# Decoder layer on one core: where four row sums and their split parts stand, and the residual rows' scaling, two blocks a step

## The chip, the cores and the metric

The kernel runs on one core of a Trainium2 chip. The metric is the device time of one execution in microseconds (us), the median of several runs. The engines are TensorE (PE, matrix products; PEld is its weight load), VectorE (DVE), ScalarE (ACT), GpSimd (POOL) and SyncE (SP, which issues most transfers).

## The reference

One layer of a decoder on 512 positions of 1024 channels, all in float32: layer norm of the input; one input projection that gives attention queries, a latent key/value, an index query, key and weights, three convolution inputs and two gates; attention over the 128 keys that the index scores choose; a gated short convolution; the two branches, gated and summed, through an output projection; layer norm; a gated feed-forward part with its own short convolution and a per-layer embedding; layer norm.

```python
h = layer_norm(x, ln_emb_g, ln_emb_b)
proj = h @ w_in
score = einsum(relu(einsum(q_idx, k_idx) * 1/8), w_idx * 8**-0.5)   # per query and key
sel = top_k(score, 128)                                             # causal keys only
...
merged = sigmoid(g_att + b0) * (att @ w_br_att) + sigmoid(g_conv + b1) * (conv_y @ w_br_conv)
h = layer_norm(2**0.25 * h + merged @ w_o, ln1_g, ln1_b)
...
```

## The kernel before

**Number format.** Every product is made as three products of a high and a low part. The high part is a rounding copy by ACT (`wh`, line 76, for weights), the low part a subtraction, raw minus high, by DVE or POOL (`wl`, line 143). A weight chunk (512 KB, 128x1024) is loaded by SP into one of four raw buffers, split three steps ahead of its use (`lead`), and used by 24 PE instructions.

**Order.** The whole order is written out by hand. `self.steps` is a list of functions; `run` goes through it. For step i it first calls `advance(i)` (loads and splits of the weight chunks that are due), then the functions in `self.preps[i]`, then the step itself; from step `side_from` on, it then gives DVE some rounds of top-k. Each engine does its instructions in the order in which they are issued here, so the list sets every engine's queue. The tiles of tag `k4` share 28 buffers of 4 KB a partition, those of tag `k2` eight of 2 KB, and PSUM has eight banks, taken in turn.

**Steps 0 to 19.** Steps 0 to 3 project the index queries (`qi`), a quarter each. Step 1 also turns the small keys (`ckT`, `kiT`, line 416) that `small_norm` in `start` makes (`kn` and `cn`, lines 400 to 406, on DVE, after a power on POOL, line 395). Steps 2 to 5 each make the index scores of two heads: PE `raw` (line 166), ACT `rl` (584), DVE `score` (586, one multiply-add for each head and block). Steps 4 and 5 also finish two chunks of the first convolution group, of which half was made in `start`; step 5 multiplies them (`cvu`, 764) and convolves (ACT taps 754, POOL sums 755, `cvt`). `at_first` is 6: step 6 is the group's third chunk (`cvy`, 771; its parts `cvT`, 773 and 774), steps 7 to 10 are the attention queries q0 to q3 (`qa`), steps 11 to 19 three more convolution groups of three chunks each. Steps 14 and 16 also make the latent keys and values, step 18 starts attention. From step 5 on DVE runs top-k (596 to 601) between the steps, four to two rounds a step.

**Steps 20 on.** Attention's eight parts, gates, and the branch products (`branch`, `br`) share these steps. From step 30 on the gates are made by a block product that needs sums and differences of quarter blocks of `h`: `hblock` holds the four blocks (rows half by channel half, 128x1024 each), `first_sum(n)` makes the four sums in place on POOL (line 795, tile `hx`), `first_parts(n)` their high part on ACT and low part on POOL (`fsh`, 801; `fsl`, through `low`, 143). The gate steps read these parts as `self.hsum`, first in step 31. POOL also issues transfers that add weights in DRAM (line 1329), from step 20 on, each behind a small token.

**The end of the attention part.** `at_slot` numbers the steps from 20 on, leaving out some of the gate steps. Its entries 18 to 23 are the branch products (2,1), (0,0), (1,0), (2,0), (3,1), (3,0): the pair is (channel group, branch). Each makes two PSUM banks of 12 matmuls; DVE multiplies each by its gate (902), and for branch 0 adds the other branch (904), after which ACT and POOL split the sum (`mT`, 906 and 907). The residual rows (`hr`, four blocks of 128 rows) are loaded at entry 17; `res_affine(b)` multiplies block b by `ge` and adds `be` (lines 1028 and 1029, two DVE passes over 128x1024). In the last branch step's preparation, `onto` copies the first half of each block into a PSUM bank by ACT (`wo`, 1047), and the output projection (`wo_half0`, 916 to 918) accumulates onto these banks, block by block.

Of the kernel before, what the change touches and what calls it, by code (L numbers as in the profile page):

```python
# [85 lines left out]
class Kern:  # L86
# [425 lines left out]
    def plan(self):  # L512
# [277 lines left out]
        def first_sum(n):  # L790

            b11, b12, b21, b22 = (self.hblock[g, h] for g in range(2) for h in range(2))
            to, x, y, op = ((b11, b11, b12, OP.subtract), (b12, b22, b12, OP.subtract),
                            (b22, b11, b22, OP.add), (b21, b22, b21, OP.subtract))[n]
            return lambda: nc.gpsimd.tensor_tensor(to, x, y, op=op)

        def first_parts(n):
            def f():
                b = self.hblock[((0, 0), (0, 1), (1, 1), (1, 0))[n]]
                hi, lo = (self.k4(f"fs{x}{n}", F32R, (P, 4, 256)) for x in "hl")  # L800
                nc.scalar.copy(hi, b)
                self.low("p", lo, b, hi)
                self.hsum[n] = [(hi[:, c], lo[:, c]) for c in range(4)]
            return f
# [157 lines left out]
        at_first = len(self.steps)  # L962
# [7 lines left out]
        at_slot, pairs = [], {}  # L970
        for i, o in enumerate(order):
# [24 lines left out]
            n = att_at.get(i)  # L996
# [1 line left out]
                fn = with_att(n, fn)  # L998
            step(fn, [w] if o[0] != "G" or k else pairs[j][:2])
        for n in range(4):  # L1000
            self.preps.setdefault((1, 1, 2, 3)[n], []).append(lambda n=n: first_sum(n)())
            self.preps.setdefault((3, 5, 7, 8)[n], []).append(first_parts(n))
        self.side_from = at_first - 1


# [20 lines left out]
        def res_affine(b):  # L1026
            t, (ge, be) = self.hr[b], self.res_affine
            nc.vector.tensor_tensor(t, t, ge, op=OP.mult)
            nc.vector.tensor_tensor(t, t, be, op=OP.add)
# [7 lines left out]
        self.preps.setdefault(at_slot[17], []).append(res_rows)  # L1037
        self.preps.setdefault(at_slot[19], []).append(res_scale)
        for b in range(NB):
            self.preps.setdefault(at_slot[(20, 21, 22, 22)[b]], []).append(lambda b=b: res_affine(b))  # L1040

        self.zps = {}

# [428 lines left out]
        n = len(those)  # L1472
# [323 lines left out]
```

## Time and profile before

| | |
|---|---|
| median of 3 runs | 749.81 us (749.81 to 750.61) |
| profiled execution, its own time | 750.77 us |
| its span | 748.8 us |
| mean granted TensorE clock | 0.993 |
| PE, DVE, ACT, POOL busy | 97%, 83%, 57%, 36% of the span |

The span runs from the first to the last instruction; the execution's own time has some 2 us around it. Timeline rows give the start in us from the span's start, the duration, engine, line, operation, written tile <- read tiles, shapes and count; in square brackets stands how long the engine was idle before and what ended that. An engine that waits inside an instruction shows a longer duration. A row of the windows gives a stretch, its length, then the busy time of each engine with its count of instructions, the granted clock of PE (1.00 is full speed), the DMA share and GB/s.

### The profile page before, as it was taken

To read this page: it belongs to the slowest core of one execution; us is meant where nothing else is said; L and a number is where in the kernel's file an instruction comes from. 1 tells how busy PE (TensorE), PEld (TensorE's weight loads), DVE (VectorE), ACT (ScalarE), POOL (GpSimd) and SP (SyncE) were. 2 spreads that over 40 slices of the span, in tenths; PEclk is the share of its full clock that TensorE was granted. 3 is DMA by queue.
4 is the path that set the end of the run, shared out by engine and by line. 5 is a ranking of instruction groups with operands and counts; after the bars stand their busy time and mean duration, and the time that the engine had idled before them with its cause. 6 is when DMAs were issued, how large, how long until landed. Compare 5 with 4: busy or idle time off the path is not lost. (4 is left out here: it accounts for less than half of the span.)

```text
span 748.8 us, 12201 instructions
## 1 busy us (share of the span) xinstructions
PE 726.5 (97%) x4399; PEld 640.0 (85%) x4399; DVE 621.7 (83%) x1045; ACT 426.3 (57%) x718; POOL 271.8 (36%) x332
## 2 busy tenths in 40 slices
PE   8989989999999999989999999999999999999995
PEld 5978868888888998768888999999999998888884
DVE  5879899985566665889998899999998899987787
ACT  5627274437766654333575666777777665665630
POOL 4345399526575841320101233433332212111002
PEclk9999999999999999999999999999999999999999
DMA  9362369869999999376998998889899869998761
GB/s 354 115 262 71 106 191 343 294 205 252 250 232 190 206 253 379 130 256 216 305 377 263 313 281 251 242 250 250 227 239 250 240 197 224 267 263 245 251 211 57
DMA packets 61867, 178.02 MB, mean 238 GB/s; under 512 B 7232, under 2 KB 7360, under 8 KB 61424
## 3 DMA queue, kind: packets, MB, share of 16 engines
q1 hardware_dynamic: 43968, 140.56, 53.6%
q0 software_dynamic: 16976, 35.27, 26.6%
q10 hardware_dynamic: 864, 1.43, 0.6%
q8 instruction: 34, 0.56, 0.3%
q14 instruction: 25, 0.20, 0.1%
HBM read 171.46 MB, written 70.78 MB: 324 GB/s over the span
## 5 line engine op out<-in xcount | busy, mean ns | idle before, releaser
L143 DVE TENSOR_TENSOR wl<-wr,wh 128x1024 fp32r<-128x1024 f32 (+1 forms) x175 | 200.8, 1163 | 44.5 <-ACT wh L76 44.0
L76 ACT CAST wh<-wr 128x1024 fp32r<-128x1024 f32 (+1 forms) x186 | 180.3, 976 | 73.0 <-DMA wr<-in_w_dn 11.9
L1453 POOL TENSOR_TENSOR behind<-token,neghalf 128x1 f32<-128x1 f32 x112 | 85.0, 873 | 240.5 <-ACT token L1452 212.0
L813 PE MATMUL ffb<-hsl,wh 128*128 128x256 f32 x304 | 86.1, 283 | 0.0
L813 PE MATMUL ffb<-hsh,wl 128*128 128x256 f32 x304 | 86.1, 283 | 0.0
L813 PE MATMUL ffb<-hsh,wh 128*128 128x256 f32 x304 | 86.1, 283 | 0.0
L813 PE MATMUL ffb<-h1T,wh 128*128 128x256 f32 x456 | 83.9, 283 | 0.0
L813 PEld LDWEIGHTS ffb<-h1T,wh 128*128 128x128 f32 x456 | 71.2, 192 | 0.2
L813 PE MATMUL ffb<-h1T,wl 128*128 128x256 f32 x228 | 64.9, 285 | 0.2 <-DVE wl L143 0.2
L813 PEld LDWEIGHTS ffb<-hsh,wh 128*128 128x128 f32 x304 | 58.4, 192 | 0.0
L813 PEld LDWEIGHTS ffb<-hsl,wh 128*128 128x128 f32 x304 | 58.4, 192 | 0.0
L813 PEld LDWEIGHTS ffb<-hsh,wl 128*128 128x128 f32 x304 | 58.4, 192 | 0.0
L1329 POOL DMA_DIRECT2D ws<-ws x38 | 41.3, 1232 | 11.2 <-issue 7.7
L813 PEld LDWEIGHTS ffb<-h1T,wl 128*128 128x128 f32 x228 | 43.7, 192 | 0.5 <-DVE wl L143 0.4
L185 POOL TENSOR_TENSOR rstd<-veps,neghalf 128x1 f32<-128x1 f32 x12 | 7.7, 644 | 97.2 <-DVE nm L208 63.8
L143 POOL TENSOR_TENSOR wl<-wr,wh 128x1024 fp32r<-128x1024 f32 x15 | 36.0, 2405 | 12.5 <-ACT wh L76 12.5
L1329 POOL DMA_DIRECT2D ws<-in_w_a x38 | 36.4, 1293 | 6.1 <-issue 3.9
L159 PE MATMUL cv<-hT,wl 128*128 128x512 f32 x80 | 31.4, 393 | 1.7 <-POOL wl L143 1.7
L157 PE MATMUL cv<-hT,wh 128*128 128x512 f32 x80 | 31.4, 393 | 0.0
L158 PE MATMUL cv<-hT,wh 128*128 128x512 f32 x80 | 31.2, 390 | 0.0
L743 DVE SCALAR_TENSOR_TENSOR ff<-c,vec,ff 128x510 f32<-128x510 f32 x38 | 28.5, 750 | 1.3
L740 ACT ACTIVATE ff<-c,vec 128x512 f32<-128x512 f32 x38 | 29.1, 810 | 0.2 <-DVE c L1374 0.2
(363 smaller groups left out, 2095.3 us busy)
## 6 DMA issues: line engine op xcount, KB each, us to landing
wr<-in_w_a SPq DMA_DIRECT2D x61, 512.0 KB, 4.4
ws<-in_w_a SPq DMA_DIRECT2D x76, 256.0 KB, 6.2
wr<-ws SPq DMA_DIRECT2D x38, 512.0 KB, 6.2
ws<-in_w_a POOLq DMA_DIRECT2D x38, 256.0 KB, 8.8
ws<-ws POOLq DMA_DIRECT2D x38, 256.0 KB, 11.1
wr<-in_w_b SPq DMA_DIRECT2D x15, 512.0 KB, 5.4
wr<-in_w_dn SPq DMA_DIRECT2D x15, 512.0 KB, 7.8
wr<-in_w_a SPq DMA_DIRECT2D x19, 256.0 KB, 6.5
```

What stands on the lines that cost most here:

```text
L76: nc.scalar.copy(hi, raw)
L143: (self.nc.vector if eng == "v" else self.nc.gpsimd).tensor_tensor(lo, raw, hi.bitcast(F32), op=OP.subtract)
L157: t.matmul(out, wh, xh, start=start, stop=False)
L158: t.matmul(out, wh, xl, start=False, stop=False)
L159: t.matmul(out, wl, xh, start=False, stop=stop)
L185: nc.gpsimd.tensor_tensor(r, v, self.neghalf, op=OP.pow)
L740: nc.scalar.activation(dst, src, AF.Identity, bias=v[:, bcol:bcol + 1], scale=v[:, wcol + 2 * tap:wcol + 2 * tap + 1])
L743: nc.vector.scalar_tensor_tensor(dst[:, 2:], src[:, :S - 2], v[:, wcol:wcol + 1], dst[:, 2:], op0=OP.mult, op1=OP.add)
L813: nc.tensor.matmul(o, l[:, c], r, start=start and c + i == 0, stop=stop and c == 3 and i == 2, skip_group_check=True)
L1329: return lambda: nc.gpsimd.dma_start(to, what, accum_op=OP.add, max_dma_last_dim=4096)
L1453: nc.gpsimd.tensor_tensor(self.sm("behind", [P, 1], bufs=2), t, self.neghalf, op=OP.mult)
```

## The change

The sums of `first_sum` move from steps 1, 1, 2, 3 to steps 5, 6, 7, 8; the parts of `first_parts` from steps 3, 5, 7, 8 to steps 15, 17, 18, 19. `res_affine` of blocks 0 and 1 is issued at entry 20 of `at_slot`, that of blocks 2 and 3 at entry 21; before, block 0 was at entry 20, block 1 at 21, blocks 2 and 3 at 22.

```diff
         for n in range(4):
-            self.preps.setdefault((1, 1, 2, 3)[n], []).append(lambda n=n: first_sum(n)())
-            self.preps.setdefault((3, 5, 7, 8)[n], []).append(first_parts(n))
+            self.preps.setdefault(at_first - 1 + n, []).append(lambda n=n: first_sum(n)())
+            self.preps.setdefault(at_first + (9, 11, 12, 13)[n], []).append(first_parts(n))
         self.side_from = at_first - 1
...
         for b in range(NB):
-            self.preps.setdefault(at_slot[(20, 21, 22, 22)[b]], []).append(lambda b=b: res_affine(b))
+            self.preps.setdefault(at_slot[20 + b // 2], []).append(lambda b=b: res_affine(b))
```

## The prediction

> **What bounds the kernel now.** I read the page's first part first, then the waits of TensorE (PE) over the whole span, then the timelines of VectorE (DVE), GpSimd (POOL) and PE around each wait, and last the granted clock in short windows.
>
> ```profile
> PE 726.5 (97%) x4399; PEld 640.0 (85%) x4399; DVE 621.7 (83%) x1045; ACT 426.3 (57%) x718; POOL 271.8 (36%) x332
> ```
>
> PE is busy for 726.5 of 748.8 us, so a change gains only by shortening PE's waits, or the stretches in which its clock is halved. In the next table the columns are who waited for whom, us in total, times, longest.
>
> ```profile
> PE ckT L416 <- DVE cn L406: 3.6, 2, 3.1
> PE wo L916 <- ACT wo L1047: 2.8, 2, 1.4
> ```
>
> The largest wait, 3.6 us for DVE's `cn` in step 1, lies right beside the row sums that the diff moves. Timeline rows (start, duration, engine, line):
>
> ```profile
> 39.11 7.82 POOL L795 TENSOR_TENSOR hx<-hx,hx 128x1024 f32<-128x1024 f32 x3
> 39.66 2.43 DVE L400 SCALAR_TENSOR_TENSOR kn<-cks,kmv,kig 128x64 f32<-128x64 f32 x1
> 42.20 2.54 DVE L403 SCALAR_TENSOR_TENSOR kn<-kn,krstd,kib 128x64 f32<-128x64 f32 x2
> 44.66 2.42 DVE L406 SCALAR_TENSOR_TENSOR cn<-cks,krstd,kvg 128x128 f32<-128x128 f32 x1
> 47.00 0.27 DVE L400 SCALAR_TENSOR_TENSOR kn<-cks,kmv,kig 128x64 f32<-128x64 f32 x1
> ...
> 47.71 0.35 DVE L406 SCALAR_TENSOR_TENSOR cn<-cks,krstd,kvg 128x128 f32<-128x128 f32 x1
> 47.13 0.33 PE L416 MATMUL ckT<-ident,cn 128*128 128x128 f32 x1 [3.10 <-DVE cn L406]
> ...
> 48.11 0.33 PE L416 MATMUL ckT<-ident,cn 128*128 128x128 f32 x1 [0.54 <-DVE cn L406]
> ```
>
> POOL's first three sums run from 39.11 to 46.93. In that time DVE's small steps of key block 2 take 2.43, 2.54 (a pair) and 2.42 us; those of block 3, just after the sums, take 0.27 to 0.35 each and 1.06 for the set (47.00 to 48.06). So one DVE instruction with operands in SBUF gets through for each sum of POOL. PE waits 3.10 and 0.54 us for the two `cn`. What it costs beside that shows in the granted clock (the column PEclk; the window before and the one of the halved clock, at two places):
>
> ```profile
> 45.80:49.20 3.40, 1.53 (x9) 1.29 (x10) 3.37 (x7) 0.62 (x2) 1.13 (x1) 1.00 1.02 418
> 49.20:52.60 3.40, 3.40 (x13) 3.40 (x12) 2.12 (x4) 0.46 (x1) 0.00 (x0) 0.50 1.01 410
> 318.80:322.30 3.50, 1.06 (x4) 0.58 (x4) 3.47 (x5) 1.18 (x2) 0.00 (x0) 1.00 0.14 55
> 322.30:325.70 3.40, 3.40 (x8) 2.68 (x9) 3.37 (x5) 0.42 (x1) 0.00 (x0) 0.50 0.24 54
> ```
>
> A window of 3.4 us in which PE was busy only 1.53 us (here) or 1.06 us (in the output projection) is followed by one at half the clock, which loses 3.4/2 = 1.7 us. The third wait beside moved work:
>
> ```profile
> 59.94 2.38 POOL L143 TENSOR_TENSOR fsl<-hx,fsh 128x1024 fp32r<-128x1024 f32 x1 [13.02 <-ACT fsh L801]
> 62.29 3.35 POOL L795 TENSOR_TENSOR hx<-hx,hx 128x1024 f32<-128x1024 f32 x1
> 60.71 0.48 ACT L146 CAST qi<-qi 128x384 fp32r<-128x384 f32 x1 [0.84 <-PE qi L159]
> 59.98 3.42 DVE L143 TENSOR_TENSOR wl<-wr,wh 128x1024 fp32r<-128x1024 f32 x1
> 63.33 0.55 DVE L147 TENSOR_TENSOR qi<-qi,qi 128x384 fp32r<-128x384 f32 x1
> 63.80 2.39 DVE L586 SCALAR_TENSOR_TENSOR score<-rl,widx,score 128x512 f32<-128x512 f32 x1
> 63.93 0.62 PE L166 MATMUL raw<-kiT,qi 64*128 64x256 f32 x5 [1.71 <-DVE qi L147]
> ```
>
> DVE's `wl` of 59.98 waits out the low part of 59.94 and takes 3.42 us, of which 1.08 are left after that low part's end at 62.32; behind it stands `qi`, whose bank PE needs: 1.71 us. Then the fourth sum holds the score product of 63.80 until 65.64.
>
> **The change, part 1: sums and low parts.** Four sums leave steps 1, 1, 2, 3 for steps 5 to 8; four pairs (high part on ACT, low part on POOL) leave steps 3, 5, 7, 8 for steps 15, 17, 18, 19. No instruction is added or removed, and none of the moved ones issues a DMA, so SP's queue keeps its order; on POOL's queue they are moved past weight low parts and convolution taps.
>
> In steps 1 to 4 they are gone. Block 2 then takes 1.06 us instead of 39.66 to 47.00, and both blocks are done near 41.8, before PE gets there at 47.13 - 3.10 = 44.03. That is 3.10 + 0.54 + 1.7 = 5.3 us. With POOL idle, `wl` takes 1.1 and `qi` waits for ACT alone, so the 1.71 go too: PE is 7.05 us earlier at the end of step 3. Both gains need POOL idle, and nothing else is in its queue there until the low part of q0 (step 4).
>
> But PE doesn't keep the 7.05, since it meets POOL again at 98.06, and that meeting hangs on DVE.
>
> ```profile
> 77.59 0.48 DVE L586 SCALAR_TENSOR_TENSOR score<-rl,widx,score 128x256 f32<-128x256 f32 x1
> 85.23 2.39 POOL L143 TENSOR_TENSOR wl<-wr,wh 128x1024 fp32r<-128x1024 f32 x1 [1.02 <-ACT wh L76]
> 85.39 2.64 DVE L586 SCALAR_TENSOR_TENSOR score<-rl,widx,score 128x384 f32<-128x384 f32 x1
> 94.36 1.30 POOL L774 TENSOR_TENSOR cvT<-cvy,cvT 128x512 fp32r<-128x512 f32 x1 [6.74 <-DMA ws<-in_w_a]
> 95.62 2.39 POOL L143 TENSOR_TENSOR wl<-wr,wh 128x1024 fp32r<-128x1024 f32 x1
> 98.06 0.50 PE L159 MATMUL qa<-hT,wl 128*128 128x512 f32 x1 [1.12 <-POOL wl L143]
> ...
> 111.29 0.50 PE L159 MATMUL cv<-hT,wl 128*128 128x512 f32 x1 [1.50 <-POOL wl L143]
> ...
> 96.48 0.43 DVE L596 MAX8 m<-tk 128x8 f32<-128x256 f32 x1
> ```
>
> Backwards: PE's third matmul of q3 (98.06) waits for POOL's `wl` (95.62 to 98.01); that stands behind `cvT` (94.36), which follows DVE's `cvy`; that stands behind the last scores (the row of 85.39 and two more) and four top-k rounds. Those scores wait, through ACT's taps, for the scores that end at 78.07. POOL then has no gap until the `wl` for which PE waits 1.50 us at 111.29. So the shift of PE behind 111 us is the shift of this chain on DVE.
>
> Up to 78.07: `qi`, now at 63.33, comes right behind ACT's copy of 60.71, so at 60.71 + 0.48 - 5.3 = 55.9: -7.4. The first score product (ended 66.19) gains the held 1.9 more. Afterwards POOL has the same number of blocks there (the low part of step 5 becomes the sum of step 5: 2.6 us, 7.82/3, against 2.4), but earlier, on top of scores that ran free before; I put the end of these scores at 70.4, so -7.7. Then step 6 has one sum more than before. It follows the `wl` of 85.23 directly, where POOL was idle for 6.74 us, so it costs POOL nothing, but it falls on the last two score products. Bounds: 0, if they get in ahead, and 2.43, the row of 39.66. I take 2.4, since in the rows above a waiting POOL instruction always went ahead of the next DVE one. Chain: -7.7 + 2.4 = -5.3. The sums of steps 7 and 8 take the places of two low parts of the same shape and fall on top-k: MAX8 at 96.48 takes 0.43 beside a running POOL `wl`, so it isn't held. Were that cover gone, each would cost up to 2.4.
>
> PE then comes to q3 at 96.94 - 7.05 = 89.9 and waits until 98.06 - 5.3 = 92.8: 2.9 us instead of 1.12. A half-clock window may follow (1.7 us); the 1.50 of wait at 111.29 swallow all but 0.2 of it. Part 1: **-5.2 us** (from -7.7 to -3).
>
> The Trainium skill (TensorE: Matmul & The Clock Gate, "HAM oscillation") asks only that PE isn't idle for more than about 3.4 us at a time. By it the 2.9 us wait would be free and the sum 0.2 us lower; the windows above differ from it, since 3.10 + 0.54 us and twice 1.42 us were enough to halve the clock, so I keep the 0.2.
>
> The low parts in steps 15 to 19 fall into POOL's gaps; the last column gives the idle time before:
>
> ```profile
> 140.72 2.47 POOL L755 TENSOR_TENSOR cvt<-cvt,tap 128x511 f32<-128x511 f32 x2 [6.49 <-ACT tap L754]
> 159.25 2.40 POOL L143 TENSOR_TENSOR wl<-wr,wh 128x1024 fp32r<-128x1024 f32 x1 [9.15 <-ACT wh L76]
> ```
>
> Four of 2.4 us are 9.6; the gaps of 6.49 and 9.15 take three, and the fourth (step 19) pushes `cvT` and the first weight additions by about 1 us. PE has no wait between 111.29 and 280, and no product needs these rows before step 31. I cost them at 0; were a gap missing, 2.4 each on POOL, with `cvt` and DVE's `cvy` queued behind. ACT, busy for 57% of the span by the first row, gets the high parts of the same steps: also 0, and less than 2.4 each, since POOL's slower pass over that tile takes as long.
>
> **Part 2: the residual rows, two blocks a step.** The passes (L1028, L1029) of blocks 0, 1 now go into branch step (1,0) and those of 2, 3 into (2,0), instead of (1,0), (2,0) and twice (3,1).
>
> ```profile
> 308.13 1.21 DVE L1028 TENSOR_TENSOR hr<-hr,ge 128x1024 f32<-128x1024 f32 x1
> 309.37 1.23 DVE L1029 TENSOR_TENSOR hr<-hr,be 128x1024 f32<-128x1024 f32 x1
> 310.51 0.69 DVE L902 TENSOR_TENSOR sig<-br,sig 128x512 f32<-128x512 f32 x1
> 311.35 0.47 PE L157 MATMUL br<-at,wh 128*128 128x512 f32 x1 [0.34 <-DVE sig L902]
> 315.77 1.10 ACT L1047 COPY wo<-hr 128x512 f32<-128x512 f32 x2
> 319.81 0.51 PE L916 MATMUL wo<-wh,mT 128*128 128x512 f32 x1 [1.42 <-ACT wo L1047]
> ...
> 327.35 0.39 PE L916 MATMUL wo<-wh,mT 128*128 128x512 f32 x1
> 305.50:311.05 5.55, 5.51 (x25) 4.23 (x23) 0.54 (x1) 1.00 0.29 96
> ```
>
> A block costs 1.21 + 1.23 = 2.44 us of DVE. They stand ahead of that step's L902, and the steps are chained (L904, ACT's `mT` and `wh`, the next `wl`, the passes, L902), so L902 of (2,0) moves from 310.51 to about 315.4. With eight PSUM banks in turn, the first bank of (3,0) is the one this L902 frees: PE waits 0.34 for it today. It would wait 0.34 + 4.88 = 5.2 us, from 311.01 to 316.2, then need 5.5 for the step (the row of 305.50) and lose 1.7 to a half-clock window: 323.4. By then ACT's four copies to `wo` are done (from 315.77 + 4.88 = 320.65, 0.55 each, end 322.9), so the two waits of 1.42 and their half-clock window are gone. The first 24 `wo` products, 0.228 apart, end at 328.9; today they end at 327.35. Part 2: **+1.5 us** (0 without the half-clock window, +2.5 with two).
>
> **Sum.** 750.77 (the profiled execution) - 5.2 + 1.5 = 747.1. The median of the runs lies 0.96 lower, 749.81, but one of three is at 750.61; taking half of this I say 746.5.
>
> **Rivals.** *A: the sum of step 6 doesn't hold the scores.* The chain keeps -7.7; PE waits 0.5 at q3: 750.8 - 7.7 + 1.5 = 744.6. For it: POOL's `wl` ends only 1 us before the last scores. Against: POOL is waiting already. The Trainium skill (SBUF — State Buffer, "Who interferes with whom") says that of the two engines the one that issues first keeps the shared ports for its whole instruction; the 3.42 of 59.98 agrees.
>
> *B: part 2 pays.* If (3,0) gets another bank, the wait of 5.2 doesn't come, and 2.84 + 1.7 us at `wo` go: 750.8 - 5.2 - 4.5 = 741.1. Against: the row of 311.35.
>
> *C: the gain is given back.* The moved sums hold as much on the DVE chain as they did in step 1 (one more or two of 2.4, in steps 7 and 8, against the MAX8 row): -5.3 becomes -2.9 or -0.5, and 750.8 - 2.9 + 1.5 = 749.4, or 751.8.
>
> *D, slower: PE's wait at (3,0).* If the wait of 4.88 us more comes with its half-clock window (1.7) and the `wo` copies still come late, it costs 6.6, with a second window 8.3: 752.2 to 753.9. It decides from 5.2, what part 1 brings. Against: the copies depend on rows that are done 6 us earlier.
>
> **How the numbers follow.** Forecast 0.45, A 0.18, B 0.10, C 0.17, D 0.10. What this kernel's runs can tell from no change is about 0.2%, 1.5 us: faster is below 748.3, slower above 751.3. Faster: nearly all of the forecast (0.44), A and B, 0.72; same: most of C (0.15), a little of the forecast and of D, 0.18; slower: the rest of C and of D, 0.10. The range leaves out B and D: 743.0 to 750.6. The forecast's own is 744.9 to 748.3.
>
> **What would show it.** Right: no `ckT` wait, no `raw` wait and no half clock near 49 us; a `qa` wait near 3 us; a `br` wait of some 5 us on L902 and none on `wo`. Wrong: a `qa` wait under 1.5 (A), no `br` wait (B), top-k instructions of 2 us (C), or both a `br` and a `wo` wait (D). A `raw` or ACT wait on a buffer that changed hands would be a cause that I haven't seen.

## The result, and the profile after

| | before | changed |
|---|---|---|
| median (lowest to highest), us | 750.21 (749.81 to 750.91) | 745.13 (744.33 to 745.23) |
| profiled execution: its time, its span, us | 750.77, 748.8 | 745.23, 743.5 |
| mean granted TensorE clock | 0.993 | 0.991 |

The changed kernel takes 0.9929 of the time of before (0.9912 to 0.9946): 5.1 us less. The first part of its page:

```profile
PE 725.6 (98%) x4399; PEld 640.4 (86%) x4399; DVE 615.6 (83%) x1045; ACT 425.6 (57%) x718; POOL 269.2 (36%) x332
```

PE's busy time is 0.9 us less, so some 4.4 of the 5.3 us of span are waits that went. PE's waits now (us in total, times, longest):

```profile
PE br L157 <- DVE sig L902: 4.7, 1, 4.7
PE qa L159 <- POOL wl L143: 2.0, 1, 2.0
...
PE cv L159 <- POOL wl L143: 0.4, 1, 0.4
```

The waits for `cn` (3.6 us in all), for `qi` (1.71) and for the `wo` copies (2.8) are not in the list any more; the last `br` wait has grown from 0.34 to 4.7 us, the `qa` wait from 1.12 to 2.0. Rows of the timeline, first the front end of the kernel:

```profile
39.92 0.28 DVE L400 SCALAR_TENSOR_TENSOR kn<-cks,kmv,kig 128x64 f32<-128x64 f32 x1
41.67 0.35 DVE L406 SCALAR_TENSOR_TENSOR cn<-cks,krstd,kvg 128x128 f32<-128x128 f32 x1
...
61.99 2.61 POOL L795 TENSOR_TENSOR hx<-hx,hx 128x1024 f32<-128x1024 f32 x1
68.15 0.49 DVE L586 SCALAR_TENSOR_TENSOR score<-rl,widx,score 128x256 f32<-128x256 f32 x1
68.29 1.49 POOL L624 TENSOR_TENSOR w_uk<-w_uk_raw,w_uk 128x512 fp32r<-128x512 f32 x1 [3.70 <-ACT w_uk L623]
68.55 2.31 DVE L143 TENSOR_TENSOR wl<-wr,wh 128x1024 fp32r<-128x1024 f32 x1
70.79 0.68 DVE L764 TENSOR_TENSOR cvu<-half,cvc 128x512 f32<-128x512 f32 x1
...
79.23 2.71 POOL L795 TENSOR_TENSOR hx<-hx,hx 128x1024 f32<-128x1024 f32 x1
77.03 5.20 DVE L586 SCALAR_TENSOR_TENSOR score<-rl,widx,score 128x384 f32<-128x384 f32 x2
82.86 0.43 DVE L596 MAX8 m<-score 128x8 f32<-128x256 f32 x1
...
89.40 2.37 POOL L143 TENSOR_TENSOR wl<-wr,wh 128x1024 fp32r<-128x1024 f32 x1
91.82 0.77 PE L159 MATMUL qa<-hT,wl 128*128 128x512 f32 x1 [2.00 <-POOL wl L143]
91.72 2.38 POOL L795 TENSOR_TENSOR hx<-hx,hx 128x1024 f32<-128x1024 f32 x1
92.26 0.43 DVE L596 MAX8 m<-tk 128x8 f32<-128x256 f32 x1
105.06 0.50 PE L159 MATMUL cv<-hT,wl 128*128 128x512 f32 x1 [0.44 <-POOL wl L143]
...
143.77 4.76 POOL L143 TENSOR_TENSOR fsl<-hx,fsh 128x1024 fp32r<-128x1024 f32 x2
...
308.71 0.68 DVE L902 TENSOR_TENSOR sig<-br,sig 128x512 f32<-128x512 f32 x1
309.54 0.76 PE L157 MATMUL br<-at,wh 128*128 128x512 f32 x1 [4.73 <-DVE sig L902]
322.49 0.39 PE L916 MATMUL wo<-wh,mT 128*128 128x512 f32 x1
```

With POOL idle the small steps of the keys take 0.28 and 0.35 us, and both `cn` are done at 42.02. From there each step of the prediction can be checked by the shift of PE: 98.06 to 91.82 is -6.24 us, 111.29 to 105.06 is -6.23. The last branch step reaches PE at 311.35 - 0.34 = 311.01 before and at 309.54 - 4.73 = 304.81 now, -6.20: nothing was lost between, so the low parts in steps 15 to 19 cost nothing. The wait of 4.73 us then takes back 4.4, and behind 24 `wo` products (327.35 to 322.49) -4.86 are left.

Two rows of before that the prediction didn't show:

```profile
79.13 0.68 DVE L764 TENSOR_TENSOR cvu<-half,cvc 128x512 f32<-128x512 f32 x1
...
89.06 0.43 DVE L596 MAX8 m<-score 128x8 f32<-128x256 f32 x1
```

`cvu` is 8.3 us earlier than before, but the first `MAX8`, behind the last scores, only 6.2: the sum of step 6 (79.23) lies on two of these scores, which take 5.20 us together; one stood beside a POOL `wl` before, too (2.64 us at 85.39), the other ran free. That is the 2.1 us between 8.3 and 6.2.

Windows of the changed kernel (stretch, length, busy time of PE, PEld, DVE, ACT and POOL with counts, granted clock, DMA share, GB/s):

```profile
88.40:91.80 3.40, 1.12 (x4) 0.30 (x2) 3.16 (x11) 3.40 (x6) 3.40 (x3) 1.00 0.25 77
91.90:95.30 3.40, 3.40 (x8) 2.71 (x9) 3.16 (x11) 3.40 (x6) 3.40 (x2) 0.50 0.65 215
306.90:310.30 3.40, 0.76 (x2) 0.70 (x3) 3.33 (x5) 0.10 (x1) 0.00 (x0) 0.50 0.00 0
310.30:313.70 3.40, 3.40 (x10) 2.63 (x9) 1.68 (x3) 2.69 (x4) 2.80 (x2) 0.50 0.02 5
```

The half clock behind the `qa` wait is hidden by the next wait: 0.44 us at `cv` instead of 1.50. The two windows behind the `br` wait are halved while PE runs from 309.54 to 313.70, which loses 4.2/2 = 2.1 us.

### The profile page after: what moved, and what is told of

It is laid out like the page before. It is cut to its first block, busy times and chain, and to the rows that moved or that the text cites. A ratio compares the mean times of both kernels' runs of the same rounds, so it can differ in the third digit from the quotient of the medians.

```text
span 743.5 us, 12196 instructions
## 1 busy us (share of the span) xinstructions
PE 725.6 (98%) x4399; PEld 640.4 (86%) x4399; DVE 615.6 (83%) x1045; ACT 425.6 (57%) x718; POOL 269.2 (36%) x332
## 3 DMA queue, kind: packets, MB, share of 16 engines
q10 hardware_dynamic: 864, 1.43, 0.6%
## 4 chain that ended last, share of the span: by engine, by line
PE 88%; DVE 6%; ACT 2%; POOL 1%; DMA 1%; issue 1%; DVEq 0%; ACTq 0%; POOLq 0%
PE ffb L813 23%; PE gtb L813 5%; PE dn L1527 5%; PE dn L1526 5%; PE dn L1528 5%; PE cv L157 2%; PE cv L159 2%; PE cv L158 2%; PE gt L157 2%; PE wo L918 2%; PE wo L917 2%; PE gt L159 2%; PE gt L158 2%; PE wo L916 2%; PE pg L1168 2%; PE pg L1169 2%
## 5 line engine op out<-in xcount | busy, mean ns | idle before, releaser
L1453 POOL TENSOR_TENSOR behind<-token,neghalf 128x1 f32<-128x1 f32 x112 | 82.3, 857 | 241.4 <-ACT token L1452 205.2
L1329 POOL DMA_DIRECT2D ws<-ws x38 | 39.3, 1170 | 11.2 <-issue 6.1
```

The lines of the kernel that those rows point to most:

```text
L1329: return lambda: nc.gpsimd.dma_start(to, what, accum_op=OP.add, max_dma_last_dim=4096)
L1453: nc.gpsimd.tensor_tensor(self.sm("behind", [P, 1], bufs=2), t, self.neghalf, op=OP.mult)
```

## The experiments

The theory: the gain is POOL's hold on DVE's short steps in front of PE, and its size is set at q3 by the chain over the scores and top-k; the price of the rows is the bank that L902 frees too late. The rivals: the gain comes from the low parts that leave steps 3 to 8; the rows cost nothing or cost by ACT's copies. Edits are against the changed kernel.

**Part 1 alone, and part 2 alone.** The rows stay as before; or the sums and parts do.

```diff
-at_slot[20 + b // 2]
+at_slot[(20, 21, 22, 22)[b]]                  # part 1 alone
...
-at_first - 1 + n / at_first + (9, 11, 12, 13)[n]
+(1, 1, 2, 3)[n]  / (3, 5, 7, 8)[n]            # part 2 alone
```

> Part 1 alone: sums and parts where the change puts them, residual rows as before. Theory (the gain is all part 1, the rows cost 1.6 us): 750.2 - 6.2 - 0.3 = 743.7 us, 1.4 us below the changed kernel; PE waits 0.3 us at the last branch step, twice 1.4 us at the output projection, with one half-clock window of 3.4 us there. Rival (the rows, two blocks a step, bring part of the gain): 745.1 us or more.

> Part 2 alone: residual rows two blocks a step, sums and parts as before. Theory: the wait for L902 at the last branch step grows to about 5 us and takes the place of the two waits at the output projection; 750.2 + 1.6 = 751.8 us, ratio 1.002. Rival (rows that are ready earlier pay): at or below 750.2 us, with no long wait at the last branch step.

Part 1 alone: 744.4 us, 0.9909 (0.9896 to 0.9921). Part 2 alone: 752.2 us, 1.0021 (1.0009 to 1.0033), so it costs 1.6 us. The product of the two ratios is 0.9930, the change's own 0.9929: within these intervals the parts add up. Part 2 alone waits as the changed kernel does at the last branch step (its row in PE's waits), and not at `wo`:

```profile
PE br L157 <- DVE sig L902: 4.7, 1, 4.7
```

With part 1 alone that wait is 0.34 again, but the `wo` waits, three with 3.4 us in all, come without the half clock expected. The windows of that run and of before tell why. Part 1 alone (PE only):

```profile
310.35:313.75 3.40, 2.01 (x10) 1.00 0.45 154
313.75:317.20 3.45, 2.02 (x8) 1.00 0.00 0
317.20:320.60 3.40, 3.40 (x17) 1.00 0.50 140
```

Before (all engines), the window ahead of the prediction's row of 45.80:

```profile
42.40:45.80 3.40, 1.63 (x11) 1.35 (x10) 3.40 (x3) 0.48 (x1) 3.32 (x2) 1.00 0.99 395
```

The grid seems fixed: the clock falls at 49.20 and 322.30 before, 273.1 us or 80 windows of 3.414 us apart. Before, both waits of 1.42 us lie in one window, which leaves PE 1.06 us of work (the prediction's row of 318.80), and the next is halved; here the two long ones (1.39 and 1.43) lie in a window each (2.01 and 2.02 us of work), and none is. There is no sharp limit in PE's busy time, as two pairs of windows show (PE only), part 2 alone and then the low parts alone:

```profile
62.30:65.70 3.40, 1.67 (x17) 1.00 0.18 58
65.75:69.10 3.35, 3.35 (x18) 0.50 0.26 98
...
42.60:46.00 3.40, 1.69 (x12) 1.00 0.97 390
46.00:49.40 3.40, 0.44 (x2) 1.00 1.04 424
```

A window with 1.67 us of work is followed by half clock, one with 1.69 is not, nor is the one with 1.63 before.

**The low parts alone.** The sums stay in steps 1, 1, 2, 3; the parts go to steps 15 to 19; the rows as before.

```diff
-preps.setdefault(at_first - 1 + n, [])        # sums
+preps.setdefault((1, 1, 2, 3)[n], [])
...
-at_slot[20 + b // 2]
+at_slot[(20, 21, 22, 22)[b]]
```

> Only the high and low parts go to steps 15 to 19; the four sums stay in steps 1 to 3, rows as before. Theory (the sums are what holds DVE): PE's wait of 3.6 us for cn and the half-clock window behind it stay, since three sums still run beside kn and cn; the 1.7 us wait for qi goes or shrinks, since the low part of step 3 is gone; 750.2 - 1.7 = 748.5 us (747 to 749). Rival (the low parts are what holds DVE): 744 to 745 us.

746.27 us, 0.9939 (0.9922 to 0.9956): the expectation missed by 2.2 us. POOL's row of this run:

```profile
39.36 10.25 POOL L795 TENSOR_TENSOR hx<-hx,hx 128x1024 f32<-128x1024 f32 x4
```

All four sums stand back to back, and the second wait for `cn` is longer, 2.69 us instead of 0.54 (5.8 in all). PE is 1.5 us later than before at the end of step 3, but 2.5 us earlier at step 12: the waits at q3 and at `cv` (1.12 and 1.50) are gone, because three low parts less stand in POOL's queue in steps 5 to 8. That I had left out. The wait for `qi` (1.71) is gone too, as the theory had it. So the rival holds a part of the truth: moving the low parts out pays 0.6% by itself, and the sums, put in their places in steps 5 to 8, bring the q3 wait back in exchange for the `cn` ones. By the shift of PE the low parts alone bring 3.0 us at 700 us, where part 1 brings 6.6.

**Sums out of top-k's way too.** Only one sum is left in steps 5 to 8; or the four sums go to DVE, with the rows as in the run below.

```diff
-at_first - 1 + n              /  at_first + (9, 11, 12, 13)[n]
+at_first + (-1, 9, 9, 11)[n]  /  at_first + (11, 13, 12, 14)[n]      # one sum left
...
-return lambda: nc.gpsimd.tensor_tensor(to, x, y, op=op)
+return lambda: nc.vector.tensor_tensor(to, x, y, op=op)              # sums on DVE
```

> As the changed kernel, but sums 1 to 3 go from steps 6 to 8 to steps 15, 15 and 17 and the parts to steps 17, 19, 18 and 20, so POOL has three blocks of 2.4 us less between the last scores and the low part of x1 (step 12). Theory (PE's shift is set by the chain from DVE's last scores over POOL's queue): no qa wait over 0.5 us and no cv wait for POOL, PE some 9.5 us ahead of the kernel before at step 12 instead of 6.2; 745.1 - 3.3 = 741.8 us. Rival (something else sets that shift, the top-k rounds on DVE or the banks): 745 us, with another wait in the place of the two.

> Rows behind the products, and the four sums on DVE itself at the same steps 5 to 8 (1.2 us each instead of 2.4 to 2.7 on POOL). Theory (a sum on POOL costs DVE its whole length, so DVE is better off doing it): the qa wait of 2.0 us shrinks, PE passes step 12 some 8 to 10 us ahead of the kernel before instead of 6.2, and against 741.6 us with the sums on POOL it is 739 to 740 us, what is left being taken at step 20 by a top-k that is no earlier. Rival (DVE is the full engine, so more work on it costs): 743 us or more.

Both missed, and both by the same thing: 747.87 us, 0.9955 (0.9942 to 0.9968), and 745.19 us, 0.9923 (0.9909 to 0.9937), where its base, the next run, has 741.57. At q3 the mechanism came out as expected: PE's shift against before is -8.28 (one sum left) and -8.23 (sums on DVE) instead of -6.24, so the sum of step 6 costs 2.0 us on POOL (those of steps 7 and 8 stand behind the low part for which q3 waits, the first at 91.72). At step 12 they lead by 10.5 and 10.4 us. They lose it at attention. One sum left, DVE, POOL and PE:

```profile
146.61 2.44 DVE L673 TENSOR_SCALAR nmx<-mx 128x8 f32<-128x8 f32 x1
...
146.60 2.42 POOL L143 TENSOR_TENSOR fsl<-hx,fsh 128x1024 fp32r<-128x1024 f32 x1
...
153.03 0.82 PE L687 MATMUL pT<-ident,p 128*128 128x128 f32 x4 [1.85 <-DVE p L679]
155.91 0.45 PE L687 MATMUL pT<-ident,p 128*128 128x128 f32 x1 [2.05 <-DVE p L679]
```

A DVE step over 128x8 that takes 0.17 us in the changed kernel (at 148.51) takes 2.44 beside the low part of step 18, which a sum moved to step 17 had pushed there; everything of the first attention part stands behind it, PE waits 3.9 us, and a window of half clock follows. Only a part of the 3.9 is this hold: with no low part there (sums clear, below) `nmx` takes 0.17 and 2.2 us of wait are left. With the sums on DVE the same place goes by DVE's own time: top-k ends later, and the waits of 4.9 us (two, longest 3.1) come with three windows of half clock:

```profile
153.30:163.50 10.20, 7.29 (x38) 5.86 (x39) 9.59 (x18) 5.26 (x9) 5.83 (x4) 0.50 0.38 136
```

The Trainium skill (SBUF — State Buffer, "Who interferes with whom") says that `tensor_scalar` can enter a mode that takes the ports shared with GpSimd, that whoever issues first then blocks the other fully, and that an instruction with at most one input from SBUF, outside such modes, does not contend. The 2.44 us agree, and so does the `MAX8` at 92.26 of the changed kernel, which has one such input and takes 0.43 beside the sum of step 7 (91.72).

**The rows behind the branch's own work.** `res_affine` is issued behind the branch step's own DVE instructions, for blocks 0 to 3 at entries 19, 20, 21, 21.

```diff
-self.preps.setdefault(at_slot[20 + b // 2], []).append(lambda b=b: res_affine(b))
+self.posts.setdefault(at_slot[(19, 20, 21, 21)[b]], []).append(lambda b=b: res_affine(b))
...
             fn()
+            for f in self.posts.get(i, ()):
+                f()
```

> As the changed kernel, but the residual passes stand behind the products' DVE steps instead of ahead: block 0 at the end of branch step (0,0), block 1 at the end of (1,0), blocks 2 and 3 at the end of (2,0), where DVE waits 1.6 us for a high part today. Theory (the cost of the rows is that L902, which frees the bank of the last branch step, stands behind them): no br wait over 0.5 us, no wo wait, no half-clock window there; against sums alone (744.4 us) the 0.34 + 2.84 + 1.7 us go: 739.5 us. Rival (the cost is DVE's load in these steps, wherever the passes stand): 744 to 745 us, with a br or wo wait of 3 us or more.

741.57 us, 0.9883 (0.9868 to 0.9898), 3.6 us under the changed kernel. The `br` wait and its half clock are gone; the `wo` waits are not. PE's waits:

```profile
PE wo L917 <- ACT wo L1048: 2.5, 2, 1.9
```

The timeline of DVE, POOL, ACT and PE around them:

```profile
305.27 2.32 DVE L1029 TENSOR_TENSOR hr<-hr,ge 128x1024 f32<-128x1024 f32 x1
...
304.82 3.93 POOL L908 TENSOR_TENSOR mT<-sig,mT 128x512 fp32r<-128x512 f32 x2 [4.34 <-ACT mT L907]
312.90 0.50 PE L917 MATMUL wo<-wh,mT 128*128 128x512 f32 x1 [0.62 <-ACT wo L1048]
...
333.19 1.14 ACT L66 CAST wh<-wr 128x512 fp32r<-128x512 f32 x2 [0.88 <-DMA wr<-in_w_b]
334.23 1.10 ACT L1048 COPY wo<-hr 128x512 f32<-128x512 f32 x2
334.86 0.50 PE L917 MATMUL wo<-wh,mT 128*128 128x512 f32 x1 [1.93 <-ACT wo L1048]
```

Behind L902 the passes meet POOL's `mT` (L908 here), and one takes 2.32 us where a free one takes 1.21; ACT's copies to `wo` stand behind them, and PE waits 0.62 for one. The longer wait, 1.93, is another one: 22 us later, in the second half of the output projection, ACT's copies stand behind splits of weights that waited for their DMA. Neither before nor the changed kernel waits there (part 1 alone waits 0.56); the lead of 10.9 us behind the first 24 `wo` products meets the loads. The expectation missed by 2.1 us: it took off 1.7 for a half clock that part 1 alone doesn't have, and it didn't have this second meeting. So what the passes cost in the changed kernel is their place in DVE's queue ahead of L902, as the prediction said.

**Banks asked for first.** The last branch step's two PSUM tiles are asked for ahead of the four `wo` tiles.

```diff
+        def first_banks():
+            self.branch_banks = [self.ps("br") for _ in range(2)]
...
-                    o = self.ps("br")
+                    o = self.branch_banks.pop(0) if self.branch_banks else self.ps("br")
...
-lambda: [onto(0, b) for b in range(NB)]
+lambda: [first_banks()] + [onto(0, b) for b in range(NB)]
```

> As the changed kernel, but the last branch step takes its two banks ahead of the four of the output projection, so they are those of branch step (0,0), long free. Theory (PE waits there for a bank and nothing else): the br wait of 4.7 us goes, and PE waits instead about 4 us at the first wo product, for ACT's copies, which stand behind the high parts of the same chain; 744.3 us (0.8 below the changed kernel, as the copies end 2.5 us before PE comes to them now, less the half clock). Rival (PE waits for DVE's data there, not for the bank): br wait unchanged, 745.1 us.

746.21 us, 0.9939 (0.9919 to 0.9958), with a `br` wait of 4.9 us: no change, and no test either. In the built program the last branch step's tiles stand in the banks of branch step (2,0) in both kernels, whatever the order of asking. That the freed thing is this bank fits those bank numbers; another bank was not tried.

**Further spread.** Three versions with the sums and parts spread beyond attention's start; the last two have the rows behind as well, and the low part of one gate chunk on DVE instead of POOL.

```diff
-at_first - 1 + n              /  at_first + (9, 11, 12, 13)[n]
+at_first + (-1, 9, 9, 13)[n]  /  at_first + (11, 16, 15, 18)[n]     # sums clear; with the rows behind: all
+at_first + (-1, 9, 9, 20)[n]  /  at_first + (11, 22, 13, 23)[n]     # spread, with the rows behind
...
-lo="p" if i < 16 else "v"
+lo="p" if i < 15 else "v"                                           # all, and spread
```

> As the run with three sums later, but the third of them in step 19 and the parts in steps 17, 22, 21, 24, so that POOL has no low part beside the first attention step's nmx and p (DVE, 146 to 156 us). Theory (there DVE lost 2.4 us to a POOL low part, and PE its lead of 10.5 us): PE keeps some 8 us at step 20, a pT wait of about 2 us is left, behind the low part of the second gate chunk; 745.1 - 2 = 743 us. Rival (top-k itself ends too late, so the lead is lost anyway): 745 us or more and pT waits of 4 us again.

> The run before this one with the residual passes behind the products, and the low part of the second gate chunk on DVE behind p instead of on POOL beside it. Theory (the gains are at different places of PE's path and add up): the pT wait goes too; 743 - 6.5 - 1.5 = 735 us (734 to 738). Rival (a lead of over 6 us is lost at the next meeting with DVE or with transfers, before 280 us): 739 to 740 us, as with the rows alone.

> Rows behind the products, and sums and parts spread over steps where DVE has no two-operand work that PE waits for: sums in steps 5, 15, 15, 26, parts in steps 17, 19, 28, 29, the low part of the second gate chunk on DVE. Theory (a POOL block costs PE only where DVE's held step is on PE's path): PE keeps some 8 to 10 us of lead to 280 us, 735 to 738 us. Rival (the lead beyond 6 us is lost anywhere between 160 and 280 us, since DVE has no slack there): 741 to 742 us, as with rows behind alone, and waits of PE for DVE or ACT between 170 and 230 us.

Sums clear: 749.29 us, 0.9986 (0.9972 to 1.0001). All: 743.91 us, 0.9915 (0.9901 to 0.9929). Spread: 739.78 us, 0.9856 (0.9843 to 0.9870). All three expectations missed (743, 735, and 735 to 738); sums clear can't be told from the kernel before. All three lead by 10.6 or 10.7 us at step 12. Sums clear loses 2.4 us of it at attention's start; then it and all lose 6 to 7 us at a place that neither before nor the changed kernel waits at. The waits of all:

```profile
PE lg L166 <- DVE sig L903: 2.3, 1, 2.3
...
PE lg L166 <- ACT pT L694: 1.0, 1, 1.0
```

The longer one ends when DVE is through with its multiply of the branch step near 192 us (`sig`), and a window of half clock follows. The traces of all, and then of spread, tell where DVE's delay starts:

```profile
177.33 3.52 POOL L143 TENSOR_TENSOR fsl<-hx,fsh 128x1024 fp32r<-128x1024 f32 x1
181.03 0.55 DVE L672 CUSTOM_DVE_ANT_0 p<-lg,madd 128x384 f32<-128x384 f32 x1 [3.24 <-PE gt L159]
191.47 0.69 DVE L903 TENSOR_TENSOR sig<-br,sig 128x512 f32<-128x512 f32 x1
...
176.49 0.56 DVE L672 CUSTOM_DVE_ANT_0 p<-lg,madd 128x384 f32<-128x384 f32 x1
186.92 0.68 DVE L903 TENSOR_TENSOR sig<-br,sig 128x512 f32<-128x512 f32 x1
```

From attention's `p` to `sig` it is 10.4 us in both; `p` itself is 4.5 us later in all, behind the low part of step 22 (177.33 to 180.85). The bracket names a gate product, but in the built program `p` waits only for its own logits, which PE ends at 175.26. Ahead of it in DVE's queue stands a token for a weight addition, which waits for POOL's `behind` (L1454), and that stands behind the low part on POOL. In spread, which moves two pairs to steps 28 and 29, PE's wait is 0.2. No run moved this low part alone. The spread version, the fastest of all, keeps 10.0 us at 180 and ends 10.7 us earlier by its span (738.1). It loses 1.2 us in the second half of the output projection, as the run with the rows behind does. PE's waits at `wo` in it:

```profile
PE wo L917 <- ACT wo L1048: 1.9, 2, 1.2
```

## Why the prediction was right, step by step

- **Steps 1 to 3.** 7.05 us were forecast; PE was 7.35 us earlier at the end of step 3. The `cn`, `raw` and half-clock terms all held.
- **The meeting at q3, the mis-sized term.** The forecast was -5.3 for the chain; it is -6.24. The scores behind the step-4 heads end at 68.64 instead of 78.07, -9.4 and not -7.7, since one POOL block that I left on them, `w_uk` (68.29), fell on DVE's `wl` of 68.55 instead. That `wl` takes 2.31 us and not 1.22, so 1.1 are paid back there and `cvu` gains 8.3. The sum of step 6 costs 2.1 (2.0 by the run with one sum left), not 2.43. The two errors, 0.6 and 0.3, have one sign; that the first is not 1.7 is luck, since the payment at `wl` wasn't foreseen. The wait is 2.00 us, not 2.9.
- **Half clock at q3.** One window came, and the second wait, 1.50 before, hid it: 0.44 is left, where 0.2 had been said to be lost. It cost nothing (-6.24 and then -6.23).
- **Low parts in steps 15 to 19, 0.** Right: -6.20 at the last branch step. But the cover is thin, and there was luck in it: `nmx` at 148.51 starts just as the low parts of steps 17 and 18 end (143.77 + 4.76 = 148.53). With a sum ahead of one of them (one sum left) `nmx` was held, and PE waited 3.9 us at attention's start.
- **Part 2, +1.5.** It is 1.6 by the run alone and 1.3 by rows (6.20 to 4.86). Against part 1 alone, whose PE leads by 7.8 us behind the same 24 products, it is 2.9 at this place: the half clock at `wo` that the prediction lets go is one of the kernel before, which part 1 alone has already lost. The wait is 4.73 of 5.2 forecast, the half clock two windows with 2.1 lost instead of 1.7; the two nearly cancel.
- **Sum.** 750.77 - 6.2 + 1.3 = 745.9; the remaining 0.6 (the profiled execution took 745.23) come mostly behind 700 us, where PE's shift is still -4.8, and were not traced. (Two of the prediction's sums are 0.1 off: -5.3 and 0.2 lost make -5.1, and 747.1 less half of 0.96 is 746.6.) Forecast 746.5, measured 745.13.
- **Rivals.** A (the sum of step 6 holds nothing): no, 2.0 to 2.1 us, though its time, 744.6, is nearer the result than the forecast; the reason is the scores, not the sum. B: no, the wait came. C: no, `MAX8` takes 0.43 beside the sum of step 7 (92.26) and the chain isn't held again. D: no, the `wo` waits are gone.

## What to carry to other kernels

A POOL block can cost DVE's next instruction up to the block's own length, so a block's place is chosen by what DVE runs beside it and who waits for that, not by how idle POOL is. Here the two-input steps (`kn`, `score`, `wl`) and the one-input `nmx` were held; `MAX8` was not, and is the cover to look for. A pass that nobody awaits belongs behind the instruction that frees a bank, not ahead of it: here that was worth 3.6 us. A lead won at one meeting of two engines is kept only if the next meeting (here attention's start, a branch step, and the weight loads of the output projection) is looked at too.

## What the runs showed of the hardware that was not expected

- A step over only 128x8 took 2.44 us (0.17 without POOL): the size of the DVE instruction doesn't bound its cost beside POOL.
- The clock halves by PE's work in a fixed window of 3.41 us, not by the length of a wait. Windows with 1.06, 1.12 and 1.53 us of work were followed by half clock, those with 2.01 and 2.02 were not; between 1.63 and 1.69 both happened. So two `wo` waits, 2.8 us together, cost a halved window before, and two of the same length none with part 1 alone. The Trainium skill (TensorE: Matmul & The Clock Gate, "HAM oscillation") speaks of idle gaps over about 3.4 us; these runs differ, since waits of 1.42 us each and of 2.00 were enough.
